# A hybrid decoder layer: adaLN weight loads on GpSimd's queue, and early-tile biases by one VectorE pass each over transposed weights, paused around two stages

## The chip, the cores and the metric

The kernel runs on one core of one Trainium2 chip. The metric is the device time of one execution in microseconds (us); the number given for a kernel is the median of three runs. Most executions of a kernel agree within 0.3%.

## The reference

One layer, one sequence of 512 tokens, width 2048, all in float32:

```python
mod = silu(c) @ w_ada + b_ada                       # w_ada is 2048 x 6144
shift, scale, gate = split(mod, 3)
h = rms_norm(x, norm_w) * (1 + scale) + shift
proj = h @ w_in                                     # q, k, v, gates, DeltaNet q/k/v, z, beta, a, merge gates
y_a = (sliding_window_attention(...) * silu(ag)) @ w_o_swa
y_b = (gated_delta_rule(...) normed * silu(z)) @ w_o_dn          # w_o_dn is 4096 x 2048
y = sigmoid(mg_a) * y_a + sigmoid(mg_b) * y_b
out = x + gate * (y @ w_out)
```

Only `c` and `w_ada` are needed for `shift`, `scale` and `gate`. The product `h @ w_in` splits into `(norm(x)*(1+scale)) @ w_in + shift @ w_in`, and the second term is one number per output channel: a bias.

## The kernel before, in words

**Matmuls.** A weight tile of 128 output channels (`raw`, 128x2048, 1 MB) is loaded by SP's queue (`load_job`, L203). `split` (L53) makes a high part on ACT (`whi`, L55) and a low part on DVE (`wlo`, L56), half a tile at a time, and `mm3` (L243 to L245) does three matmuls of 128x512 per 128 input channels: high by high, high by low, low by high. The hidden state lies in SBUF as `hh` and `hl`. `channel_tile` does one such tile: 48 matmuls, with a call of `pump` after every sixth.

**Startup (L345 to L555).** The four `x` tiles are loaded (L367). Thirty-two tiles of `w_ada` (`wa`, 1 MB each, six buffers that the `x` tiles use too) are loaded by SP (L359), and each gives 128 values of `scale` (the first 16) or `shift` (the last 16), in `ada_sum`: for tiles 0, 1, 23, 25, 27 and 29 by matmuls on PE (L413, L419), otherwise by one DVE pass (L422). `high` makes the hidden channels (ACT L443, L444) and `low` their remainder (DVE L448).

The projections begin before the shift is known. In the loop over the 16 blocks of input channels nine output tiles at once (two value tiles `v`, seven tiles `b` of the branch-b merge gate; weights `w_st`) are made from the state without shift, so they lack their bias. `store` copies each out of PSUM on ACT (L514) and SP writes it to DRAM (L515). Two more unshifted tiles follow (mb5 and mb6, here called so by their place), and beside them the last twelve `ada_sum`s, stepped by `pump`. Then the whole state is made again with the shift (DVE L438, ACT L444, DVE L448), and the tile `ba` (weights `w_tr`, with a `k` tile beside it) is the first that uses it.

**Order.** A tile scheduler turns the program into one queue of instructions per engine, and each engine runs its queue in order. Next to the tiles, generators are stepped by `pump`: those in `live` with a delay, those in `slow` with a budget (the first DeltaNet solve, `s0`, 0.88 per call), and those in `side` at a rate per call.

**Branch b (L1033 to L1070).** For each half of 4096 channels the DeltaNet output is read back from DRAM in 16 tiles (`oraw`, two buffers, L1048) and split into `oh` (ACT L55) and `ol` (DVE L56); meanwhile PE does two merge-gate tiles, and then 16 tiles `od` follow. Side work at rate 0.36 comes first from `shift_products`, then from `gate`. `shift_products` makes the missing biases of the nine early tiles: it loads the same weights again (`sw`, L1532; for the first tiles in pieces of 512 bytes a packet), multiplies by the shift on POOL (L1537), sums over the 16 blocks on DVE (L1542) and over partitions by a 128x1 matmul (L1545, L1548). `gate` loads 16 tiles `gw` (L1561) and accumulates them on DVE (L1567), then sums over partitions on PE (L1575) and DVE (L1576). Both share one buffer for `sw` and `gw`.

Of the kernel before, what the change touches and what calls it, by code (L numbers as in the profile page):

```python
# [7 lines left out]
F32 = mybir.dt.float32  # L8
# [8 lines left out]
P = 128  # L17
# [22 lines left out]
class Layer:  # L40
# [239 lines left out]
    def build(self):  # L280
        tc, nc, a = self.tc, self.nc, self.a
        with ExitStack() as es:
# [12 lines left out]
            self.hold, self.keep_order = 0, False  # L295
# [49 lines left out]
    def startup(self, st):  # L345
# [9 lines left out]
        def load_ada(n):  # L355
            if n >= 2 * KT:
                return
            wa = s2.tile([P, D], F32, tag="wa", name="wa", bufs=6)
            nc.sync.dma_start(out=wa, in_=a["w_ada_ss"][n // KT, n % KT])  # L359
            loads[n] = wa  # L360
# [151 lines left out]
        def store(ps, dst):  # L512
            t = s2.tile([P, T], F32, tag="h32", name="raw")
            nc.scalar.copy(out=t, in_=ps)  # L514
            nc.sync.dma_start(out=dst, in_=t)  # L515
# [128 lines left out]
    def deltanet(self):  # L644
# [9 lines left out]
        with ExitStack() as ps:  # L654
# [4 lines left out]
            with ExitStack() as sa:  # L659
# [9 lines left out]
                s0 = self.paced(self.solve(sol0, 0, nc.vector), 0.88)  # L669
# [363 lines left out]
    def branch_b(self):  # L1033
        tc, nc, a = self.tc, self.nc, self.a
        with ExitStack() as es:
# [5 lines left out]
            self.beside(self.shift_products(wk, pg), 0.36, "gate")  # L1041
            self.beside(self.gate(wk, pg), 0.36, "gate")
            oh = op.tile([P, KT, T], F32R, name="oh")
            ol = op.tile([P, KT, T], F32R, name="ol")
            for half in range(2):
# [6 lines left out]
                for j in range(KT):  # L1052
                    ps = self.channel_tile(f"od{half}_{j}", oh, ol)
                    y = wk.tile([P, T], F32, tag="yb", name="yb", bufs=3)
                    if half == 0:
                        nc.scalar.copy(out=y, in_=ps)
                    else:
# [3 lines left out]
                        if j < NPRE:  # L1061
                            nc.scalar.activation(th, th, AF.Tanh, scale=0.5, bias=self.bias_h[:, j : j + 1])
# [54 lines left out]
    def attention(self):  # L1117
        tc, nc, a = self.tc, self.nc, self.a
        with ExitStack() as es:
# [7 lines left out]
            for i in range(2):  # L1127
                t = keep.tile([P, T], F32, name=f"vch{i}")
                nc.sync.dma_start(out=t, in_=self.v_d[i])
                nc.scalar.activation(t, t, AF.Identity, bias=self.bias_v[:, i : i + 1])  # L1130
# [388 lines left out]
    def shift_products(self, wk, pp):  # L1519

        nc, a = self.nc, self.a
        st = a["w_st"].rearrange("u p (b c) -> p u b c", b=2)
        src = [st[:, :, :, i * P : (i + 1) * P] for i in range(2 + NST)] + [a["w_ch"][96 + j] for j in range(NST, NPRE)]
        ps = pp.tile([P, T], F32, tag="g", name="pshift")
        for _ in range(7):
            yield
        for n, w_d in enumerate(src):
            w = wk.tile([P, D], F32, tag="gw", name="sw", bufs=1)
            if n < 2 + NST:
                wb = w.rearrange("p (u b c) -> p u b c", b=2, c=P)  # L1530
                for b in range(2):
                    nc.sync.dma_start(out=wb[:, :, b, :], in_=w_d[:, :, b, :])  # L1532
            else:
                nc.sync.dma_start(out=w, in_=w_d)
            yield
            wv = w.rearrange("p (k c) -> p k c", c=P)
            nc.gpsimd.tensor_tensor(  # L1537
                out=wv, in0=wv, in1=self.shift.unsqueeze(2).to_broadcast([P, KT, P]), op=ALU.mult
            )
            yield  # L1540
            r = wk.tile([P, P], F32, tag="sr", name="sr", bufs=2)
            nc.vector.tensor_reduce(out=r, in_=w.rearrange("p (k c) -> p c k", c=P), axis=AX.X, op=ALU.add)  # L1542
            yield
            if n:
                nc.tensor.matmul(ps[:, n - 1 : n], lhsT=last, rhs=self.ones[:, 0:1], start=True, stop=True)  # L1545
            last = r
        yield
        nc.tensor.matmul(ps[:, n : n + 1], lhsT=last, rhs=self.ones[:, 0:1], start=True, stop=True)  # L1548
        self.bias_v = self.const.tile([P, 2], F32, name="bias_v")
        nc.vector.tensor_copy(out=self.bias_v, in_=ps[:, 0:2])  # L1550
        self.bias_h = self.const.tile([P, NPRE], F32, name="bias_h")
        nc.vector.tensor_scalar(out=self.bias_h, in0=ps[:, 2 : 2 + NPRE], scalar1=0.5, scalar2=None, op0=ALU.mult)
        yield

    def gate(self, wk, pp):

        nc, a = self.nc, self.a
        acc = wk.tile([P, D], F32, name="gate_bc", bufs=1)
# [23 lines left out]
def layout(i):  # L1582
# [21 lines left out]
    o["w_ch"] = f(np.concatenate([ch(w_in[:, 4608:16896]), ch(w_in[:, 19008:]), ch(w_in[:, :2304]), ch(w_in[:, 2560:4608]), ch(w_in[:, 16960:19008])]))  # L1604
    o["w_os"] = f(ch(i["w_o_swa"][0]))
# [57 lines left out]
```

## Time and profile before

| what | value |
|---|---|
| median of 3 runs | 2981.06 us (2978.43 to 2982.47) |
| profiled execution | 2980.36 us |
| its span in the trace | 2978.6 us |
| PE busy | 2887.3 us (97%) |
| DVE, ACT, POOL busy | 1858.3, 1099.8, 272.8 us |
| DMA | 460.57 MB, mean 155 GB/s |

A row of a group reads: line, engine, operation, result and operands, shape, count, then busy time, mean duration, and the time for which the engine sat idle just before, with what ended it. Matmuls overlap in the pipe, so that the duration of one (some 0.39 us) is longer than the distance between the starts of two.

### The profile page before, as it was taken

Reading aid. Unit: us, or ns where it says so; the run is one execution under the profiler, and the core shown is the slowest. Engines: PE = TensorE matmul, PEld = TensorE weight load, DVE = VectorE, ACT = ScalarE, POOL = GpSimd, SP = SyncE. Lnnn points to the kernel's source line nnn. Section 1 sums busy time; section 2 is a strip of 40 time slices with the busy share of each in tenths; the row PEclk is TensorE's granted clock in tenths of the full one; section 3 lists DMA queues with packets and bytes.
Section 4 is the critical chain, followed back from the end, with each engine's and each line's share of the span. In section 5 each row is a group of like instructions: output and inputs, shape, how many; then the busy total and the mean of one; then the engine's idle time right before and its main releaser. Section 6 shows DMA issues by size and latency. Waiting matters only on the chain.

```text
span 2978.6 us, 38106 instructions
## 1 busy us (share of the span) xinstructions
PE 2887.3 (97%) x14506; PEld 2362.3 (79%) x14506; DVE 1858.3 (62%) x2962; ACT 1099.8 (37%) x2136; POOL 272.8 (9%) x213
## 2 busy tenths in 40 slices
PE   8888999899999999999999989999999999999988
PEld 7767788788888888888888778788788878778867
DVE  7676799677777544555554454553656556554697
ACT  5244433334334433333333322321234434432333
POOL 0002121121000000001000021000000000000011
PEclk9989999999999999999999999999999999999999
DMA  9746654643333533343332556865332223275563
GB/s 365 280 145 183 185 165 158 195 129 119 120 123 111 160 107 125 112 133 116 125 115 96 170 187 216 277 228 169 105 112 86 88 90 99 95 248 179 183 193 92
DMA packets 189897, 460.57 MB, mean 155 GB/s; under 512 B 72689, under 2 KB 89585, under 8 KB 153745
## 3 DMA queue, kind: packets, MB, share of 16 engines
q1 hardware_dynamic: 189714, 458.14, 46.6%
q8 instruction: 114, 1.87, 0.3%
q14 instruction: 69, 0.57, 0.1%
HBM read 396.39 MB, written 59.45 MB: 153 GB/s over the span
## 4 chain that ended last, share of the span: by engine, by line
PE 75%; DVE 7%; DMA 5%; issue 2%; ACT 2%; POOL 1%; SPq 0%; POOLq 0%; DVEq 0%; ACTq 0%
PE mm L243 21%; PE mm L245 21%; PE mm L244 21%; DMA oraw<-o_d 2%; DMA gw<-in_w_ada_gate 2%; DVE wlo L56 2%; PE S L1264 1%; PE pv L969 1%; PE po L988 1%; PE O L1315 1%; PE pP L277 1%; PE po L987 1%; PE pd L984 1%; PE pp L959 1%; DVE sr L1542 1%
## 5 line engine op out<-in xcount | busy, mean ns | idle before, releaser
L243 PE MATMUL mm<-hh,whi 128*128 128x512 f32 x2752 | 1120.5, 407 | 6.4 <-DVE yq L634 5.5
L245 PE MATMUL mm<-hh,wlo 128*128 128x512 f32 x2752 | 1079.7, 392 | 1.8 <-DVE wlo L56 1.8
L244 PE MATMUL mm<-hl,whi 128*128 128x512 f32 x2752 | 1077.4, 392 | 0.2 <-DVE hl L56 0.2
L56 DVE TENSOR_TENSOR wlo<-raw,whi 128x1024 fp32r<-128x1024 f32 (+1 forms) x452 | 559.9, 1242 | 449.8 <-ACT whi L55 445.2
L55 ACT CAST whi<-raw 128x1024 fp32r<-128x1024 f32 (+1 forms) x452 | 470.4, 1043 | 961.0 <-PE mm L244 874.8
L243 PEld LDWEIGHTS mm<-hh,whi 128*128 128x128 f32 x2752 | 519.7, 189 | 114.6 <-issue 14.3
L245 PEld LDWEIGHTS mm<-hh,wlo 128*128 128x128 f32 x2752 | 517.6, 188 | 114.3 <-DVE wlo L56 2.6
L244 PEld LDWEIGHTS mm<-hl,whi 128*128 128x128 f32 x2752 | 519.6, 189 | 98.8 <-issue 0.8
L244 PE MATMUL mm<-ol,whi 128*128 128x512 f32 x512 | 202.5, 397 | 6.3 <-DVE ol L56 6.3
L243 PE MATMUL mm<-oh,whi 128*128 128x512 f32 x512 | 203.5, 399 | 3.8 <-ACT oh L55 3.8
L245 PE MATMUL mm<-oh,wlo 128*128 128x512 f32 x512 | 201.8, 396 | 4.9 <-DVE wlo L56 4.9
L916 POOL TENSOR_TENSOR qe<-qe,yq 128x512 f32<-128x512 f32 x32 | 50.7, 1602 | 904.0 <-DMA qe<-eg_rows 786.4
L765 POOL TENSOR_TENSOR E<-E,neg_g 128x512 f32<-128x512 f32 x64 | 79.7, 1247 | 519.3 <-DMA E<-g_rows 262.5
L244 PEld LDWEIGHTS mm<-ol,whi 128*128 128x128 f32 x512 | 97.6, 191 | 31.0 <-DVE ol L56 10.1
L245 PEld LDWEIGHTS mm<-oh,wlo 128*128 128x128 f32 x512 | 97.7, 191 | 27.2 <-DVE wlo L56 7.1
L243 PEld LDWEIGHTS mm<-oh,whi 128*128 128x128 f32 x512 | 97.3, 190 | 26.5 <-ACT oh L55 5.4
L808 DVE TENSOR_TENSOR atmp<-A 128x62 f32<-128x62 f32 (+30 forms) x124 | 111.0, 895 | 1.4
L815 DVE TENSOR_TENSOR A<-A,atmp 128x62 f32<-128x62 f32 (+30 forms) x124 | 110.9, 894 | 1.5
L962 DVE SCALAR_TENSOR_TENSOR r<-pp,neg_eg,vt 128x128 f32<-128x128 f32 x96 | 29.2, 346 | 78.9 <-PE pp L959 77.6
L1288 ACT ACTIVATE sm<-sm,mx,rs 128x256 f32<-128x256 f32 (+1 forms) x128 | 71.7, 562 | 3.9 <-DVE mx L1283 3.9
L634 DVE SCALAR_TENSOR_TENSOR yv<-mm,convh,yv 128x511 f32<-128x511 f32 (+2 forms) x96 | 71.4, 744 | 1.6
L422 DVE SCALAR_TENSOR_TENSOR wa<-wa,silu_cb 128x2048 f32<-128x2048 f32 x26 | 59.4, 2284 | 5.9 <-DMA wa<-in_w_ada_ss 5.9
(351 smaller groups left out, 3320.6 us busy)
## 6 DMA issues: line engine op xcount, KB each, us to landing
raw<-in_w_ch SPq DMA_DIRECT2D x156, 1024.0 KB
wa<-in_w_ada_ss SPq DMA_DIRECT2D x32, 1024.0 KB
raw<-in_w_od SPq DMA_DIRECT2D x32, 1024.0 KB
E<-g_rows SPq DMA_DIRECT2D x64, 256.0 KB
gw<-in_w_ada_gate SPq DMA_DIRECT2D x16, 1024.0 KB
raw<-in_w_os SPq DMA_DIRECT2D x16, 1024.0 KB
qe<-eg_rows SPq DMA_DIRECT2D x32, 256.0 KB
o_d<-zh SPq DMA_DIRECT2D x32, 256.0 KB
```

What stands on the lines that cost most here:

```text
L55: self.nc.scalar.copy(out=hi, in_=src)
L56: self.nc.vector.tensor_tensor(out=lo, in0=src, in1=hi.bitcast(F32), op=ALU.subtract)
L243: nc.tensor.matmul(ps, lhsT=wh, rhs=xh, start=first, stop=False)
L244: nc.tensor.matmul(ps, lhsT=wh, rhs=xl, start=False, stop=False)
L245: self.last_mm = nc.tensor.matmul(ps, lhsT=wl, rhs=xh, start=False, stop=last).ins
L422: nc.vector.scalar_tensor_tensor(out=wa, in0=wa, scalar=1.0, in1=scb, op0=ALU.mult, op1=ALU.mult, accum_out=acc)
L634: nc.vector.scalar_tensor_tensor(out=y[:, s:], in0=ps[:, : T - s], scalar=w[:, j : j + 1], in1=y[:, s:], op0=ALU.mult, op1=ALU.add)
L765: nc.gpsimd.tensor_tensor(out=E, in0=E, in1=ng, op=ALU.add)
L808: eng.tensor_tensor(out=t, in0=A[:, m : m + 1, m + 1 :].to_broadcast([P, m, n]), in1=A[:, :m, m : m + 1].to_broadcast([P, m, n]), op=ALU.mult,
L815: eng.tensor_tensor(out=A[:, :m, m + 1 :], in0=A[:, :m, m + 1 :], in1=t, op=ALU.add)
L916: nc.gpsimd.tensor_tensor(out=qf, in0=qf, in1=q, op=ALU.mult)
L1288: nc.scalar.activation(t, t, AF.Exp, scale=r[:, h : h + 1], bias=mx[:, h : h + 1], accum_out=den[:, h : h + 1])
```

## The change

1. The 32 loads of `wa` are issued by GpSimd (POOL) and not by SP.
2. The nine stores of early tiles are issued by ACT and not by SP.
3. The budget of `s0` is 0.85 for 0.88.
4. `pump` skips side work while a flag `side_held` is set: from the start of branch b until its first tile `od0_0` has been done, and from `od0_15` until `od1_0` has been done. Between, the rate is 0.28 for 0.36.
5. `shift_products` is another computation. Sixteen 128x128 matmuls and four ACT copies spread the shift as a row over all partitions (`row`, in the buffer that `gate` accumulates in afterwards). Then each of the nine tiles is loaded from a copy of the weights with output channels on partitions (`w_early`, 128x2048, 8 KB in a row), and one DVE pass multiplies by the row and accumulates to one column of `bias`. POOL's multiplications, DVE's reductions and the 128x1 matmuls are gone.

```diff
@@ pump
-            if not q:
+            if not q or self.side_held:
                 continue
@@ startup: load_ada, store
-            nc.sync.dma_start(out=wa, in_=a["w_ada_ss"][n // KT, n % KT])
+            nc.gpsimd.dma_start(out=wa, in_=a["w_ada_ss"][n // KT, n % KT])
...
-            nc.sync.dma_start(out=dst, in_=t)
+            nc.scalar.dma_start(out=dst, in_=t)
@@ deltanet
-                s0 = self.paced(self.solve(sol0, 0, nc.vector), 0.88)
+                s0 = self.paced(self.solve(sol0, 0, nc.vector), 0.85)
@@ branch_b
-            self.beside(self.shift_products(wk, pg), 0.36, "gate")
-            self.beside(self.gate(wk, pg), 0.36, "gate")
+            row = wk.tile([P, D], F32, name="gate_bc", bufs=1)
+            self.beside(self.shift_products(wk, pg, row), 0.28, "gate")
+            self.beside(self.gate(wk, pg, row), 0.28, "gate")
...
+            self.side_held = True
...
                     ps = self.channel_tile(f"od{half}_{j}", oh, ol)
+                    self.side_held = j == KT - 1
@@ shift_products
+        for q in range(4):
+            ps = pp.tile([P, 4, P], F32, tag="g", name="pshift")
+            for c in range(4):
+                w = self.shift[:, 4 * q + c : 4 * q + c + 1].to_broadcast([P, P])
+                nc.tensor.matmul(ps[:, c, :], lhsT=w, rhs=self.ident, start=True, stop=True)
+            nc.scalar.copy(out=row[:, q * T : (q + 1) * T], in_=ps.rearrange("p c n -> p (c n)"))
             yield
+        bias = self.bias = self.const.tile([P, 2 + NPRE], F32, name="bias")
+        for n in range(2 + NPRE):
             w = wk.tile([P, D], F32, tag="gw", name="sw", bufs=1)
+            nc.sync.dma_start(out=w, in_=a["w_early"][n])
             yield
+            nc.vector.scalar_tensor_tensor(
+                out=w, in0=w, scalar=1.0, in1=row, op0=ALU.mult, op1=ALU.mult, accum_out=bias[:, n : n + 1]
+            )
             yield
```

Rows of the order read: line, operation, result and operands, shape, and how many follow each other. The first place is startup. Here is SP's queue of the kernel before at the end of the loop over the 16 blocks; `wa` are the adaLN tiles, `raw` of L203 the weights of coming tiles, `v_d` and `mb_d` the stores of early tiles:

```order
L203 DMA raw<-in_w_ch 128x2048
L359 DMA wa<-in_w_ada_ss 128x2048 x4
L515 DMA v_d<-raw 128x512 x2
L203 DMA raw<-in_w_tr 128x1536
L515 DMA mb_d<-raw 128x512 x2
L359 DMA wa<-in_w_ada_ss 128x2048
L515 DMA mb_d<-raw 128x512 x2
L359 DMA wa<-in_w_ada_ss 128x2048
L515 DMA mb_d<-raw 128x512
L359 DMA wa<-in_w_ada_ss 128x2048 x3
```

Now SP's queue in startup holds weights alone, from its sixth row on:

```order
L203 DMA raw<-in_w_st 128x1792 x2
L338 DMA convh<-in_conv_w 128x256
L326 DMA dnw<-in_dn_norm_w 128x1
L203 DMA raw<-in_w_st 128x1792 x6
L203 DMA raw<-in_w_ch 128x2048 x2
L203 DMA raw<-in_w_tr 128x1536 x2
L203 DMA raw<-in_w_ch 128x2048 x3
```

The stores went to ACT's queue, and all 32 loads of `wa` stand in a row in POOL's, ahead of its first work on `E` (L765). On ACT itself, in the same loop, the casts `whi` of the next weights stood behind several blocks of hidden channels (`h_...` and `hh`) in a row before:

```order
L55 COPY whi<-raw 128x896
L443 ACTIVATE h_511<-xnT,scale 128x512
L55 COPY whi<-raw 128x896
L444 COPY hh<-h_511 128x512
L443 ACTIVATE h_545<-xnT,scale 128x512
L444 COPY hh<-h_545 128x512
L443 ACTIVATE h_581<-xnT,scale 128x512
L444 COPY hh<-h_581 128x512
L443 ACTIVATE h_615<-xnT,scale 128x512
L444 COPY hh<-h_615 128x512
L443 ACTIVATE h_651<-xnT,scale 128x512
L444 COPY hh<-h_651 128x512
```

Now a cast follows each one or two blocks:

```order
L443 ACTIVATE h_511<-xnT,scale 128x512
L444 COPY hh<-h_511 128x512
L55 COPY whi<-raw 128x896
L443 ACTIVATE h_545<-xnT,scale 128x512
L444 COPY hh<-h_545 128x512
L55 COPY whi<-raw 128x896
L443 ACTIVATE h_581<-xnT,scale 128x512
L444 COPY hh<-h_581 128x512
L55 COPY whi<-raw 128x896
L443 ACTIVATE h_615<-xnT,scale 128x512
```

PE's queue has all four late `ada` groups (tiles 23, 25, 27, 29) inside mb5 and mb6; before, two of the four stood behind mb6. The second place is the beginning of branch b, on DVE. Before, the reductions of `shift_products` (L1542) stood between the splits `ol` of the read-back tiles:

```order
L56 TENSOR_TENSOR ol<-oraw,oh 128x512
L1542 TENSOR_REDUCE sr<-sw 128x128
L56 TENSOR_TENSOR ol<-oraw,oh 128x512
L56 TENSOR_TENSOR wlo<-raw,whi 128x1024
L56 TENSOR_TENSOR ol<-oraw,oh 128x512 x2
L56 TENSOR_TENSOR wlo<-raw,whi 128x1024
L56 TENSOR_TENSOR ol<-oraw,oh 128x512 x2
L1542 TENSOR_REDUCE sr<-sw 128x128
L56 TENSOR_TENSOR wlo<-raw,whi 128x1024
L56 TENSOR_TENSOR ol<-oraw,oh 128x512 x3
L1542 TENSOR_REDUCE sr<-sw 128x128
```

Now the first pass of `shift_products` (L1537) comes behind the last of the sixteen `ol`:

```order
L56 TENSOR_TENSOR ol<-oraw,oh 128x512 x2
L56 TENSOR_TENSOR wlo<-raw,whi 128x1024
L56 TENSOR_TENSOR ol<-oraw,oh 128x512 x6
L56 TENSOR_TENSOR wlo<-raw,whi 128x1024 x3
L1537 TENSOR_SCALAR sw,bias<-sw,gate_bc 128x2048
L56 TENSOR_TENSOR wlo<-raw,whi 128x1024 x2
L1537 TENSOR_SCALAR sw,bias<-sw,gate_bc 128x2048
```

On SP the same: of the nine loads of `sw` one still stands among the first half's sixteen loads of `oraw`, where there were eight of the half-tile pieces of `sw` before. In the second half three loads of `gw` stand between the first `oraw` and the last, as before, and three loads of `yb` that stood behind them now stand among them.

More of the change, by code (lines that the diff above doesn't have):

```diff
@@ L1517, in output, with shift_products @@
             evict(*f)
-    def shift_products(self, wk, pp):
+    def shift_products(self, wk, pp, row):
         nc, a = self.nc, self.a
[L1522 to L1525, printed above, removed]
+        for q in range(4):
[4 more added lines that the diff above has]
+            nc.scalar.copy(out=row[:, q * T : (q + 1) * T], in_=ps.rearrange("p c n -> p (c n)"))
@@ L1543, in shift_products @@
[L1543 to L1552, printed above, removed]
@@ L1553, in shift_products, with gate @@
-        yield
-    def gate(self, wk, pp):
+        nc.vector.tensor_scalar(out=bias[:, 2:], in0=bias[:, 2:], scalar1=0.5, scalar2=None, op0=ALU.mult)
+    def gate(self, wk, pp, acc):
         nc, a = self.nc, self.a
-        acc = wk.tile([P, D], F32, name="gate_bc", bufs=1)
         for kt in range(KT):
```

20 lines of the change are left out of this document (5 added, 15 removed).

## The prediction

> **What bounds the kernel now.** The page comes first: its busy times, and the granted clock in the forty slices.
>
> ```profile
> PE 2887.3 (97%) x14506; PEld 2362.3 (79%) x14506; DVE 1858.3 (62%) x2962; ACT 1099.8 (37%) x2136; POOL 272.8 (9%) x213
> PEclk9989999999999999999999999999999999999999
> DMA  9746654643333533343332556865332223275563
> ```
>
> PE is busy 97% of the span, so what an edit can win is PE's idle time, some 90 us, and what it can cost is work put into PE's stream. The change touches two stages, startup and branch b. I cut the span there and read PE's busy time and its count of matmuls in each stretch. The columns are the stretch, its length, then busy time and count of PE, PEld, DVE, ACT and POOL, the granted clock, the DMA share and GB/s.
>
> ```profile
> 28.50:58.50 30.00, 29.99 (x159) 24.47 (x160) 26.66 (x38) 13.03 (x19) 0.00 (x0) 1.00 1.01 415
> 58.50:70.00 11.50, 8.59 (x25) 6.21 (x24) 11.46 (x15) 6.82 (x10) 0.00 (x0) 0.70 0.66 261
> 70.00:112.50 42.50, 42.50 (x189) 35.21 (x188) 35.41 (x43) 15.71 (x21) 0.00 (x0) 1.00 0.86 344
> 112.50:137.40 24.90, 24.90 (x166) 19.66 (x164) 11.95 (x16) 6.16 (x10) 0.00 (x0) 1.00 0.40 137
> 137.40:158.80 21.40, 5.09 (x69) 4.03 (x68) 8.25 (x12) 2.88 (x6) 0.00 (x0) 0.56 0.99 381
> 158.80:186.20 27.40, 26.09 (x98) 17.16 (x99) 24.06 (x39) 12.47 (x21) 0.00 (x0) 0.84 0.26 84
> ...
> 1697.00:1740.00 43.00, 33.49 (x127) 24.83 (x125) 25.99 (x19) 10.84 (x15) 7.53 (x3) 0.92 0.60 183
> 1740.00:1885.00 145.00, 143.04 (x637) 118.21 (x636) 75.02 (x41) 37.71 (x46) 22.18 (x6) 1.00 0.63 216
> 1885.00:1940.00 55.00, 47.85 (x187) 36.11 (x186) 34.55 (x33) 17.84 (x25) 0.00 (x0) 0.94 0.83 292
> ```
>
> The stretch from 70 to 112.5 has no gap: 42.5 us for 189 matmuls, 0.225 us each. At that pace the others should last 25 x 0.225 = 5.6 (a loss of 5.9 us), 98 x 0.225 = 22.0 (5.4), 127 x 0.225 = 28.6 (14.4), 637 x 0.225 = 143.3 (1.7) and 187 x 0.225 = 42.1 (12.9). From 137.4 to 158.8 only matmuls of `ada` run, and all 21.4 us are lost. Together 61.7 us lie where the change reaches.
>
> Why the 21.4? Windows of 10 us around it, and what SP's queue did there:
>
> ```profile
> 120.00:130.00 10.00, 10.00 (x73) 7.92 (x73) 5.36 (x8) 0.75 (x2) 0.00 (x0) 1.00 0.07 27
> 130.00:140.00 10.00, 7.45 (x61) 5.52 (x59) 2.41 (x4) 3.29 (x6) 0.00 (x0) 1.00 0.63 204
> 140.00:150.00 10.00, 2.52 (x34) 2.01 (x34) 3.86 (x5) 2.02 (x4) 0.00 (x0) 0.50 0.96 351
> ```
>
> ```profile
> 126.38 7.02 SPq L515 DMA_DIRECT2D mb_d<-raw  x2
> 133.51 0.37 SPq L359 DMA_DIRECT2D wa<-in_w_ada_ss  x1
> 135.03 1.41 SPq L515 DMA_DIRECT2D mb_d<-raw  x2
> 136.53 0.46 SPq L359 DMA_DIRECT2D wa<-in_w_ada_ss  x1
> 140.79 0.32 SPq L515 DMA_DIRECT2D mb_d<-raw  x1
> 141.20 1.36 SPq L359 DMA_DIRECT2D wa<-in_w_ada_ss  x3
> ```
>
> From 120 to 130 the DMA engines stood at 0.07 while PE was full: SP held the stores of early tiles, which wait for ACT's copy, and the `wa` loads behind them could not be issued. When they were (133 to 145), PE had run out. So the queue's order made this gap, not the bytes. The waits over startup (engine and line, what it waited for, us in total, times, longest) say the same for SP, and those of PE name what came late:
>
> ```profile
> SPq L515 <- ACT raw L514: 31.4, 7, 15.5
> ...
> PE ada L413 <- DMA wa<-in_w_ada_ss: 12.0, 2, 6.0
> PE v L243 <- ACT whi L55: 1.9, 1, 1.9
> ...
> POOL E L765 <- DVE ss L713: 214.7, 1, 214.7
> ```
>
> **The change part by part**, against the profiled execution (2980.36 us; its span is 2978.6, and the median of the three runs, 2981.06, lies 0.7 above it).
>
> *The start.* With `wa` on a second queue its first two tiles come beside the four `x` tiles, 2 MB more at 0.415 MB/us (the window at share 1.01): up to 4.8 us later for the last `x`. But an `x` tile costs PE some 3.7 us and the chain is PE's and ACT's:
>
> ```profile
> 15.82 7.38 PE L471 MATMUL xtp<-dg,xt 128*128 128x128 f32 x64 [0.59 <-ACT xnT L476]
> 17.47 1.91 ACT L456 ACTIVATE hl<-xt 128x2048 fp32r<-128x2048 f32 x1
> ```
>
> ACT took the last `x` at 17.47, when four MB from 3 us on had been due at about 13. So 4 us of the delay are covered: I take +1.5, between 0 and +5.
>
> *58.5 to 70.* PE waits here for casts of weights, which stood on ACT behind five blocks of hidden channels; those wait for the `scale`s of late `wa`. Weights and `wa` now have queues of their own, and casts alternate with blocks. DVE was busy 11.46 of 11.5 here and 26.66 of 30 ahead of it, so part of the loss can stay on DVE: per block it owes one pass of `ada_sum`, a remainder and one split of 896 columns.
>
> ```profile
> L56 DVE TENSOR_TENSOR wlo<-raw,whi 128x1024 fp32r<-128x1024 f32 (+1 forms) x452 | 559.9, 1242 | 449.8 <-ACT whi L55 445.2
> ...
> L422 DVE SCALAR_TENSOR_TENSOR wa<-wa,silu_cb 128x2048 f32<-128x2048 f32 x26 | 59.4, 2284 | 5.9 <-DMA wa<-in_w_ada_ss 5.9
> ```
>
> That is 2.28 and 1.24 x 896 / 1024 = 1.09, with 0.69 for the remainder (row below) and some 0.3 of small pieces, 4.4 us, against 21 matmuls x 0.225 = 4.7 on PE: it fits, with little over. I take -4.5 (0 to -5.9).
>
> *Two groups of `ada` move ahead*, into mb5 and mb6. Before, they ran in the gap, where they cost nothing. One group shifts the stream around it by 1.1 us, and its column sum by some 0.4 (four starts late by 0.1 each), so +3.0 for two (2.2 to 3.4):
>
> ```profile
> 130.83 0.39 PE L245 MATMUL mm<-hh,wlo 128*128 128x512 f32 x1
> 131.15 1.08 PE L413 MATMUL ada<-wa,silu_cr 128*32 128x128 f32 x32
> 132.16 0.50 PE L243 MATMUL mm<-hh,whi 128*128 128x512 f32 x1
> ```
>
> *The gap.* Up to the tile `ba` startup loads 36 tiles of `wa` and `x` (1.05 MB), 8 of `w_st` (0.92), 2 of `w_ch` and 2 of `w_tr` (0.79), 48.8 MB; at 0.415 MB/us that is 118 us, ahead of mb6's end near 137. A `wa` also needs a free buffer: the last one takes that of the sixth sum before it, in the middle of mb6, near 126, and lands near 130. DVE must do eight passes of 2.28 us beside mb5 and mb6 (18 of 25 us, with four more in place of the gap's), which fits by little. What then stays is the way from the last sum through DVE (0.54), ACT (0.62) and PE (rows below): 2 us. So -19.4, between -12 (the last sums spill over by three DVE passes and a landing) and -21.4.
>
> *The tile `ba`.* Its 27.4 us hold 24.06 us of DVE, that is the rebuilt state:
>
> ```profile
> L448 DVE TENSOR_TENSOR hl<-h,hh 128x512 fp32r<-128x512 f32 x16 | 10.4, 686 | 1.5 <-ACT hh L444 1.5
> ...
> L438 DVE TENSOR_SCALAR h<-xnT,scale,shift 128x512 f32<-128x512 f32 x16 | 8.1, 540 | 0.0
> ...
> L444 ACT CAST hh<-h 128x512 fp32r<-128x512 f32 x16 | 9.3, 617 | 12.3 <-DVE h L438 12.3
> ```
>
> DVE can't do this much faster than 24, but a part of it may begin under mb6, and the clock need not recover from 0.56. I take -2.5 (0 to -5).
>
> *The stores on ACT* take its queue some 0.4 us each (row at 140.79: 0.32), 3.6 us in all, where ACT has 6.16 busy of 24.9; uncovered they would delay casts by those 3.6. *POOL's 32 loads* stand ahead of its first multiplication, which waits until 214.7 us anyway, long after the last load: nothing.
>
> *Branch b, first half.* The loss of 14.4 belongs to the read-back tiles, for which ACT and behind it DVE wait:
>
> ```profile
> ACT oh L55 <- DMA oraw<-o_d: 29.0, 11, 8.3
> ...
> L55 ACT CAST oh<-oraw 128x512 fp32r<-128x512 f32 x32 | 19.7, 620 | 58.8 <-DMA oraw<-o_d 58.6
> ...
> L1542 DVE TENSOR_REDUCE sr<-sw 128x128 f32<-128x2048 f32 x9 | 34.2, 3802 | 25.5 <-POOL sw L1537 24.1 <-PE pshift L1545 1.4
> L1567 DVE SCALAR_TENSOR_TENSOR gate_bc<-gw,silu_c,gate_bc 128x2048 f32<-128x2048 f32 x12 | 28.2, 2352 | 35.5 <-DMA gw<-in_w_ada_gate 35.5
> ```
>
> Three reductions of 3.8 us stood between the `ol`, and eight pieces of `sw` between the loads; all but one load go. Eight pairs of `oraw` with two buffers then take perhaps 3.7 us each (0.5 MB at 0.415, two casts of 0.62, and the issue), 30 us, while PE has two merge tiles (21.6) and then follows block by block: about 3 us of loss stay. Sixteen fp32 matmuls for the shift row are new on PE: 32 passes, at 7.38 / 64 each, 3.7 us. So -14.4 + 3 + 3.7 = -8 (-3 to -12). *Between the halves* nine DVE passes (2.28 by the nearest row, of `wa`, or 2.35 by the one above) replace nine of 3.80, but nothing waits for them: 0 (-2 to +2). *Second half.* The scheduler puts three `gw` loads and three DVE passes between the `oraw` as before, and three `yb` loads (0.75 MB) more, so the pause is not one in the queues: -1 (-5 to +5).
>
> *The solve at 0.85* moves steps by at most half a tile and ends in the same phase: 0 (-2 to +3).
>
> Sum: 1.5 - 4.5 + 3.0 - 19.4 - 2.5 - 8 - 1 = -30.9, and 2980.4 - 30.9 = **2949.5 us**.
>
> **The rivals.**
>
> *Bytes, not order.* If the transfers of both queues only share what one queue had, the idle 0.93 of the window from 120 to 130 (9.3 us) is all that comes back of the gap, and the loss at 58.5 stays: 1.5 + 3.0 - 9.3 - 8 - 1 = -13.8, 2966.6 us. Against it: the share of 0.07. For it: shares of 1.01 and 0.99 on either side. The Trainium skill, in "DMA: Bandwidth & Descriptors", section "Issuing engines are not separate DMA queues", speaks for it: transfers issued by any engine run on the same 16 DMA engines and interleave, and a second issuer saves only the time to initiate, usually small. The row of 31.4 us on SP disagrees in this kernel: what is saved is the wait of an issue that blocks others.
>
> *Slower: loads from POOL come one at a time.* The trace has no load from POOL. If each of the 32 takes T us from 3 us on, with no overlap, the last lands at 3 + 32 T. Before it landed near 156, so T = 4.8 gives the old gap, and with the 9 us of branch b the kernel breaks even at T = 5.1. At T = 6 the last lands at 195, +39 on the gap: 2980.4 + 39 - 9 = 3010 us. Against it: 1 MB is 2.4 us at 0.415 MB/us, so T must be double. For it: the loads have to share with as many bytes of weights. On the price there are two statements in the Trainium skill. "DMA: Bandwidth & Descriptors", section "Anatomy of one DMA — SWDGE (gpsimd) path", fits 2.0 us plus the bytes at 436 GB/s for one load from GpSimd, an estimated 4.4 us here; one at a time that gives 144 for the last and about 2957 us. "SBUF — State Buffer", section "SBUF: two separate sides", warns that GpSimd can't write descriptors while DVE runs a two-port operation; DVE's work here is mostly two-input passes (L422, L448, L56), and no run so far shows the effect.
>
> *Branch b gives nothing.* The one `sw` load and `yb`, `gw` loads keep their place, two buffers of `oraw` are slow by themselves, and the shift row costs its 3.7: 2949.5 + 9 = 2958.5. For it: the second half, with no `sw` at all, lost 12.9 us, and half of the 58.6 us that `oh` waited fell there.
>
> *All stalls go.* The gap closes entirely (2 more), the loss at 58.5 and in `ba` too (1.4 and 2.5), the start costs nothing (1.5), and branch b loses nothing (3, and 5 in the second half): 2949.5 - 15.4 = 2934.
>
> **How the numbers follow.** Forecast 0.48, branch b nothing 0.18, all stalls go 0.15, bytes 0.12, one at a time 0.07. The range of 2932 to 2968 us takes in the first four but for their tails (0.10), and leaves out the last: 0.83 inside. About 0.2%, or 6 us, is what a measurement of this kernel can tell from no change. Faster by more 0.88 (the first four but 0.05), within it 0.05, slower 0.07.
>
> **What would show it.** In the trace after: no row of SP that waits for L514; the DMA share from 120 to 130 well over 0.07, and PE without a gap of over 5 us between the last early tile and `ba`; the loss near 60 us under 2 us; 16 `oh` casts of the first half waiting less than 15 us for `oraw` in place of 29. I am wrong if `wa` loads land over 4.8 us apart, if the gap stays over 10 us with the DMA engines full, or if DVE is what PE waits for beside mb5 and mb6.

## The result, and the profile after

The changed kernel took 2958.54 us (median of 4 runs, 2954.88 to 2960.22) against 2980.34 us before (4 runs): a ratio of 0.9925, with a 95% interval of 0.9908 to 0.9942. That is 21.8 us faster, where 30.9 were forecast. The profiled execution took 2958.96 us, its span is 2957.2.

PE's time is the page's first row again, with 3.7 us less busy time and 21.4 us less span:

```profile
PE 2883.6 (98%) x14520; PEld 2362.0 (80%) x14520; DVE 1834.1 (62%) x2970; ACT 1105.7 (37%) x2140; POOL 244.9 (8%) x236
```

The same stretches as in the prediction, cut at the same events in the new trace (columns as there):

```profile
0.00:35.00 35.00, 25.36 (x226) 24.33 (x226) 19.34 (x76) 19.57 (x28) 4.45 (x12) 0.90 0.93 357
35.00:111.50 76.50, 76.50 (x345) 63.24 (x339) 76.03 (x96) 35.24 (x48) 11.85 (x23) 1.00 1.00 404
111.50:122.60 11.10, 11.10 (x78) 8.89 (x76) 5.55 (x7) 2.21 (x3) 1.06 (x2) 1.00 1.02 414
122.60:131.50 8.90, 0.42 (x3) 0.05 (x1) 1.22 (x2) 2.99 (x6) 0.00 (x0) 0.79 0.58 218
131.50:150.90 19.40, 19.40 (x156) 14.64 (x156) 7.83 (x14) 2.96 (x6) 0.00 (x0) 0.83 0.36 122
150.90:177.10 26.20, 24.28 (x102) 15.79 (x101) 21.91 (x36) 13.69 (x22) 0.00 (x0) 1.00 0.25 79
...
1693.60:1726.60 33.00, 30.89 (x146) 24.61 (x145) 12.72 (x15) 14.18 (x22) 0.00 (x0) 1.00 0.59 193
1726.60:1868.60 142.00, 142.00 (x632) 117.75 (x631) 72.68 (x56) 36.52 (x44) 0.00 (x0) 1.00 0.71 249
1868.60:1920.00 51.40, 46.65 (x193) 37.58 (x192) 29.18 (x28) 17.97 (x25) 0.00 (x0) 0.93 0.85 299
```

The loop over input channels now starts at 35 us and not at 28.5, and runs to 111.5 without a gap, with the DMA engines (1.00) and DVE (76.03 of 76.5) full. Of the gap of 21.4 us ahead of `ba` some 2 us are left. But a new one has come, 8.9 us inside mb5, followed by a slow clock (0.83). The first half of branch b loses little now: at 0.225 us each its 146 matmuls come to 32.9 of its 33.0 us.

To see where time was won and given back I compared the start of the same matmul in both traces. Each column is an event; the first row is its time before, the second how much later (+) or earlier (-) it came after:

| | first `v` | end of loop | end of mb6 | first `ba` | last `ba` | near 600 | first `od` | 4th `od` tile | end of half 1 | start of half 2's tiles | end of branch b |
|---|---|---|---|---|---|---|---|---|---|---|---|
| before, us | 28.5 | 112.3 | 137.1 | 158.9 | 184.6 | 598.7 | 1697.0 | 1745.6 | 1887.6 | 1947.3 | 2102.5 |
| after | +6.5 | -1.0 | +13.8 | -6.0 | -9.1 | -3.3 | -3.4 | -12.7 | -17.9 | -21.4 | -21.4 |

So startup won 9.1 us, the DeltaNet stage gave 5.8 back, and branch b won 18.

**The start.** ACT's first two passes over `x` wait longer, and PE's transposes with them. ACT of the changed kernel:

```profile
9.75 1.91 ACT L456 ACTIVATE hl<-xt 128x2048 fp32r<-128x2048 f32 x1 [6.83 <-DMA xt<-in_x]
...
14.45 1.91 ACT L456 ACTIVATE hl<-xt 128x2048 fp32r<-128x2048 f32 x1 [1.25 <-DMA xt<-in_x]
```

The first pass came at 6.89 before, so the first `x` tile explains 2.9 of the 6.5 us. PE meanwhile ran out of other work, stood for 4.6 us from 9.6 on, and its clock fell. PE from 10 to 20 us, before and after:

```profile
10.00:20.00 10.00, 9.04 (x77) 8.68 (x76) 7.38 (x38) 8.62 (x12) 0.00 (x0) 1.00 1.03 421
10.00:20.00 10.00, 5.75 (x32) 5.65 (x32) 4.37 (x24) 8.58 (x12) 0.00 (x0) 0.66 1.02 418
```

**The new gap.** PE's queue and ACT's at that place. Each row is start, duration, engine, line, and in brackets the idle time before with what ended it:

```profile
122.24 0.50 PE L243 MATMUL mm<-hh,whi 128*128 128x512 f32 x1
122.58 0.40 PE L244 MATMUL mm<-hl,whi 128*128 128x512 f32 x1
131.45 0.59 PE L419 MATMUL ada<-pick,adas 128*128 128x1 f32 x2 [8.47 <-ACT adas L418]
```

```profile
108.41 0.35 ACTq L515 DMA_DIRECT2D v_d<-raw  x1
108.80 0.59 ACT L514 COPY raw<-v 128x512 f32<-128x512 f32 x1 [0.42 <-PE v L245]
109.41 0.33 ACTq L515 DMA_DIRECT2D v_d<-raw  x1
116.76 0.59 ACT L514 COPY raw<-b 128x512 f32<-128x512 f32 x1 [7.38 <-DMA v_d<-raw]
...
122.04 0.59 ACT L514 COPY raw<-b 128x512 f32<-128x512 f32 x1 [3.15 <-DMA v_d<-raw]
...
128.17 0.59 ACT L514 COPY raw<-b 128x512 f32<-128x512 f32 x1 [3.09 <-DMA mb_d<-raw]
...
131.13 0.27 ACT L418 COPY adas<-ada 128x128 f32<-128x128 f32 x1 [0.40 <-ACT raw L514]
```

The issue of a store costs ACT 0.33 us, as costed. But the copies have two buffers, and the third copy waits for the first store to land: issued at 108.41, landed by 116.76, while the loads of both other queues fill the DMA engines (1.02). ACT takes its instructions in order, so the small copy `adas`, ready at 122.3, stands until 131.13 behind the copy that has just begun, three more of them and one cast, and PE stands behind `adas`.

**GpSimd's loads.** One takes POOL 0.53 us to issue, and they overlap: the median is 9.1 us from issue to landing, and at the end of the loop they go out 2.2 to 3.5 us apart.

```profile
92.45 0.53 POOL L359 DMA_DIRECT2D wa<-in_w_ada_ss  x1 [3.41 <-DVE wa L422]
94.66 0.53 POOL L359 DMA_DIRECT2D wa<-in_w_ada_ss  x1 [1.68 <-DVE wa L422]
98.12 0.53 POOL L359 DMA_DIRECT2D wa<-in_w_ada_ss  x1 [2.93 <-DVE wa L422]
```

In the loop nearly all of POOL's waiting (62.9 us in 21 waits) is for DVE to free a buffer. So the rival of loads one at a time (4.8 us each and more) is out.

**Branch b.** The reductions of 3.8 us have become passes of 2.29, and in the first half (1680 to 1740) ACT waits 9.2 us for read-back tiles in place of 29.0:

```profile
L56 DVE TENSOR_TENSOR ol<-oraw,oh 128x512 fp32r<-128x512 f32 x32 | 21.2, 689 | 21.6 <-ACT oh L55 21.6
L1537 DVE SCALAR_TENSOR_TENSOR sw<-sw,gate_bc 128x2048 f32<-128x2048 f32 x9 | 20.6, 2291 | 18.0 <-DMA sw<-in_w_early 14.5 <-ACT gate_bc L1530 3.5
```

```profile
ACT whi L55 <- PE mm L244: 21.9, 9, 4.7
ACT oh L55 <- DMA oraw<-o_d: 9.2, 5, 2.9
```

The mean of `ol` itself went from 838 to 689 ns. But no `ol` of before took 838: thirty took 0.67 to 0.69 us, as now, and two took 3.26 and 2.96. This is the second of them, on DVE of the kernel before:

```profile
1726.77 2.96 DVE L56 TENSOR_TENSOR ol<-oraw,oh 128x512 fp32r<-128x512 f32 x1 [4.99 <-ACT oh L55]
1729.65 3.79 DVE L1542 TENSOR_REDUCE sr<-sw 128x128 f32<-128x2048 f32 x1
```

POOL multiplied for the old bias from 1725.57 to 1729.18 and, beside the other one, from 1692.92 to 1697.30. Three passes `wlo` met such a multiplication too, and took 2.86 to 3.79 us for 1.22. All five ended the same time behind POOL's end, 0.55 us for `ol` and 1.08 for `wlo`, whenever they had begun: in this trace a DVE pass of these kinds stands still until POOL's instruction has ended. The same holds, with the same 0.55 and 1.08 us, for all five such meetings in each of four runs below that keep the old computation (startup only, `wa` on GpSimd only, stores on ACT only, pause only). PE's waits from 1680 to 1740, of which 4.5 us were for `ol` before, have shrunk to one of 2.1:

```profile
PE mm L244 <- DVE ol L56: 4.5, 4, 1.5
```

```profile
PE mm L243 <- ACT oh L55: 2.1, 1, 2.1
```

### The profile page after: what moved, and what is told of

The parts are those of the page before. It is cut to its first block, busy times and chain, and to the rows that moved or that the text cites. A ratio compares the mean times of both kernels' runs of the same rounds, so it can differ in the third digit from the quotient of the medians.

```text
span 2957.2 us, 38131 instructions
## 1 busy us (share of the span) xinstructions
PE 2883.6 (98%) x14520; PEld 2362.0 (80%) x14520; DVE 1834.1 (62%) x2970; ACT 1105.7 (37%) x2140; POOL 244.9 (8%) x236
## 4 chain that ended last, share of the span: by engine, by line
PE 79%; DVE 6%; DMA 3%; ACT 2%; issue 1%; POOL 1%; SPq 0%; POOLq 0%; DVEq 0%; ACTq 0%
PE mm L243 23%; PE mm L245 22%; PE mm L244 22%; DVE wlo L56 2%; DMA oraw<-o_d 1%; PE S L1267 1%; PE pv L969 1%; PE po L988 1%; PE O L1318 1%; PE pP L277 1%; PE pd L984 1%; PE pp L959 1%; PE po L987 1%; DMA qe<-eg_rows 1%; PE m L244 0%
## 5 line engine op out<-in xcount | busy, mean ns | idle before, releaser
L56 DVE TENSOR_TENSOR wlo<-raw,whi 128x1024 fp32r<-128x1024 f32 (+1 forms) x452 | 552.4, 1224 | 470.1 <-ACT whi L55 445.8
L243 PEld LDWEIGHTS mm<-hh,whi 128*128 128x128 f32 x2752 | 520.9, 189 | 116.7 <-issue 15.2
L765 POOL TENSOR_TENSOR E<-E,neg_g 128x512 f32<-128x512 f32 x64 | 76.5, 1196 | 404.3 <-DMA E<-g_rows 266.8
```

The lines of the kernel that those rows point to most:

```text
L56: self.nc.vector.tensor_tensor(out=lo, in0=src, in1=hi.bitcast(F32), op=ALU.subtract)
L243: nc.tensor.matmul(ps, lhsT=wh, rhs=xh, start=first, stop=False)
L765: nc.gpsimd.tensor_tensor(out=E, in0=E, in1=ng, op=ALU.add)
```

## The experiments

The theories. A: startup lost what was missing to two new stalls, `x` sharing the transfer rate with the first adaLN tiles, and ACT's queue standing at copies that wait for stores to land. B: the stall in mb5 is one of late adaLN tiles. C: the start is late since a load from GpSimd is slow by itself. D and E: the DeltaNet stage gave 5.8 us back by chance of the clock, or through the solve budget of 0.85. F and G: branch b won by the cheaper bias computation, or by the pauses. Medians before were 2981.03, 2980.59 and 2981.17 us in the three groups of runs. The table gives the same landmarks, in us against the profile before:

| | us, ratio [interval] | first `v` | end of loop | end of mb6 | last `ba` | near 600 | end of branch b |
|---|---|---|---|---|---|---|---|
| the change | 2958.54, 0.9925 [0.9908, 0.9942] | +6.5 | -1.0 | +13.8 | -9.1 | -3.3 | -21.4 |
| own store buffers | 2954.15, 0.9910 [0.9896, 0.9924] | +6.2 | -1.4 | +7.3 | -15.6 | -11.0 | -26.1 |
| five `wa` buffers | 2957.97, 0.9923 [0.9910, 0.9937] | +6.3 | -1.2 | +11.8 | -10.5 | -8.8 | -27.2 |
| first two `wa` by SP | 2956.66, 0.9919 [0.9905, 0.9933] | +1.6 | -4.2 | +11.6 | -11.3 | -9.9 | -27.9 |
| branch b only | 2960.61, 0.9938 [0.9925, 0.9952] | -0.1 | -1.4 | -1.4 | -2.6 | -2.2 | -24.3 |
| startup only | 2972.42, 0.9981 [0.9972, 0.9990] | +6.4 | -1.1 | +13.4 | -9.0 | -9.6 | -8.1 |
| `wa` on GpSimd only | 2970.50, 0.9971 [0.9959, 0.9982] | +7.2 | -0.3 | +12.1 | -9.4 | -10.9 | -11.0 |
| stores on ACT only | 2972.59, 0.9976 [0.9966, 0.9985] | +0.1 | +0.3 | +4.3 | -6.2 | -9.8 | -12.2 |
| both repairs | 2943.22, 0.9876 [0.9862, 0.9889] | +0.1 | -5.8 | +3.2 | -19.7 | -15.2 | -36.2 |
| budget 0.88 | 2953.86, 0.9915 [0.9902, 0.9927] | +7.1 | -0.4 | +13.9 | -9.0 | -10.2 | -26.4 |
| both repairs, 0.88 | 2940.16, 0.9865 [0.9851, 0.9879] | -0.3 | -6.2 | +0.3 | -22.1 | -23.1 | -42.7 |
| new bias, no pause | 2964.69, 0.9948 [0.9934, 0.9962] | +0.1 | -1.1 | -1.1 | -1.6 | +1.4 | -14.5 |
| pause only | 2978.61, 0.9997 [0.9989, 1.0006] | -0.2 | -1.3 | -1.4 | -2.3 | -1.8 | -3.1 |

Unchanged stages differ by up to 3 us between profiles, so differences of less in a column prove nothing alone. Single runs of one kernel differ by 2 to 15 us, and a profile is one run: those of branch b only and of the first two `wa` by SP lay 6.8 and 4.7 us under their medians.

**Own store buffers, and its control.** In the changed kernel:

```diff
+            own = len(stored) % 3 < 2
+            stored.append(0)
-            t = s2.tile([P, T], F32, tag="h32", name="raw")
+            t = s2.tile([P, T], F32, tag="st" if own else "h32", name="raw", bufs=4 if own else 2)
...
-            wa = s2.tile([P, D], F32, tag="wa", name="wa", bufs=6)
+            wa = s2.tile([P, D], F32, tag="wa", name="wa", bufs=5)
```

> The changed kernel, with six buffers for the nine stores of early tiles (four of their own and the two they had) and, since SBUF has no room for them beside it, five buffers for the adaLN tiles in place of six. Theory A: the stall of 8.9 us behind 122.6 us comes from ACT's queue, which stands still at the copies of the early tiles until earlier stores have landed (7.4 us the longest), so that the small copy that PE waits for comes late. With more buffers the stall goes, and the slow clock behind it: 2945 to 2950 us, the wait of PE on the copy of ada under 1 us. Theory B: PE waits because the last adaLN tiles and their DVE passes are late; then the stall stays or grows with one buffer less: 2958 to 2965 us.

The control has the last two lines alone (and the same for `xt`).

> The changed kernel with five buffers for the adaLN tiles in place of six, and nothing else: the control of the run with own store buffers. Theory A: the second adaLN tile is loaded only when the first x tile is free, so the start has less beside it and gains some 2 us, while the stall behind 122.6 us stays: 2954 to 2960 us. Theory B (late adaLN tiles): the depth of the loads is what counts, 2962 us or more.

With its own buffers ACT reaches `adas` at 121.96, and PE's wait for it is not in the list any more. What is left there is another wait, of PE for DVE, to free the one PSUM tile of `ada`:

```profile
PE ada L413 <- DVE shift L431: 3.8, 2, 3.6
PE ba L243 <- ACT hh L444: 1.7, 1, 1.7
PE mm L245 <- DVE wlo L56: 1.6, 1, 1.6
```

In the control it stands as in the changed kernel:

```profile
PE ada L419 <- ACT adas L418: 6.9, 1, 6.9
PE ba L243 <- ACT hh L444: 1.7, 1, 1.7
```

So theory A holds for this stall, and B falls for it, since one buffer less for adaLN tiles did not make it worse. But the wait that is left is of theory B's kind. DVE of the run with own store buffers:

```profile
131.52 2.29 DVE L422 SCALAR_TENSOR_TENSOR wa<-wa,silu_cb 128x2048 f32<-128x2048 f32 x1 [4.43 <-DMA wa<-in_w_ada_ss]
...
134.73 0.21 DVE L431 TENSOR_SCALAR shift<-ada,b_adaT 128x1 f32<-128x1 f32 x1
```

The pass that frees the tile stands on DVE behind one that waits for a late adaLN tile. With five buffers the last two tiles landed at 131.5 and 135.6, and at 124.5 and 127.5 in the changed kernel, so this may be the price of the buffers taken. From the end of the loop to that of mb6 the time fell from +14.8 to +8.7 us, the control's is +13.0. The total was 2954.15, short of the 2945 to 2950 expected: of the 11.8 us over the forecast (+3.0) the stores had 6.1, and late adaLN tiles stand next in line. The control's total fits theory A, but not the 2 us at the start that it had promised.

**First two adaLN loads by SP**, in the changed kernel:

```diff
-            nc.gpsimd.dma_start(out=wa, in_=a["w_ada_ss"][n // KT, n % KT])
+            (nc.sync if n < 2 else nc.gpsimd).dma_start(out=wa, in_=a["w_ada_ss"][n // KT, n % KT])
```

> The changed kernel with the first two of the 32 adaLN loads issued by SP behind the x tiles, as before, and the other thirty by GpSimd. Theory A: the first projection matmul came 6.5 us later than before (35.1 us) since two adaLN tiles took half the transfer rate from the x tiles; it comes back to 28 to 30 us. If the loop over input channels is bound by what it has to load (DMA share 1.0), it gives a part back: 2953 to 2958 us. Theory C: the late start is one of GpSimd's slower first loads and not of sharing: then the first matmul stays near 35 us and the time at 2958.

The first `v` came at +1.6 us for +6.5, and the loop's end at -4.2 for -1.0, so two thirds of it lasted: the late start was the order of the first loads. The edit alone does not part sharing from slow first loads of GpSimd (theory C), since both go with it, but the traces do. In the changed kernel GpSimd's first two tiles landed at 9.30 and 14.25, and PE needs the first at 27.7; what came late was `x`. The control with five buffers has only one adaLN tile beside the `x` tiles and still started at +6.3: its first `x` came at 9.36, PE stood for 3.7 us, and from 10 to 20 the clock was 0.66 there too (0.83 with the first two loads by SP). So theory A holds, but the second adaLN tile adds little: one beside the first `x` is enough to run PE dry and slow its clock. The median, 2956.66, lies in theory A's range and can't be told from the changed kernel's by itself.

**Both parts of startup, together and apart**, each on the kernel before:

> The kernel before with the two edits of startup alone: all 32 adaLN loads by GpSimd, the nine stores by ACT; branch b and the solve budget as before. Theory A (the startup edits win 9 us by the end of the tile ba and the stages behind them keep that, since they are the same code): 2971 us. Theory D (part of it is given back in the DeltaNet stage, where gaps of PE of some 3 us lie otherwise against the times at which the clock is judged; the changed kernel lost 5.7 us of 9 there): 2975 to 2980 us, with the granted clock under 1.00 somewhere between 230 and 400 us.

> The kernel before with the 32 adaLN loads by GpSimd alone; the nine stores stay on SP. Theory A: ACT's copies still wait for the landing of earlier stores, and SP's stores wait for ACT's copies with weights queued behind them, so a stall between the early tiles stays: the gap ahead of ba is short, the stall near 122 us between 4 and 12 us, 2968 to 2976 us. Rival: with no store on ACT the stall near 122 us is gone, and the gap ahead of ba too: 2962 to 2966 us.

> The kernel before with the nine stores by ACT alone; all loads stay on SP. Theory A: SP no longer stands still between 112 and 140 us, so the adaLN loads come early and most of the gap of 21.4 us closes, with no extra load beside the x tiles at the start: 2960 to 2968 us. Rival: what closed the gap is the second queue for loads, and without it the adaLN loads stand behind weights of later tiles as before: 2975 to 2982 us.

Together they won 8.2 us, apart 10.1 and 8.0: either edit alone does what both do. Startup only came out by theory A (2971), not D (2975 to 2980): its -9.0 at the last `ba` is -9.6 near 600. With the stores on ACT and all loads still on SP, the first two stores land in 4 us and not 8, SP no longer waits for ACT's copies, and the loads come early (the DMA share from 120 to 130 is 1.01, where it was 0.07); so it isn't the second queue for loads that closed the gap, but that a store which waits no longer stands ahead of loads. They are not free of the stores, though: four loads of `wa` still waited 23.8 us in all on SP for events that the profile puts down to landings of `mb_d`; why is not shown. With the loads alone on GpSimd the wait for `adas` stays (6.7 us), since ACT's copies wait for landings whoever issues them: the rival of 2962 to 2966 failed. Theory A's own figure for the stores alone (2960 to 2968) was too good as well: the gap ahead of `ba` closed to 2 us (from +4.3 at the end of mb6 to -15.4 at the first `ba`), but the tile itself then waited for its state and gave 9 us back (-6.2 at its end). PE in that stretch:

```profile
PE ba L243 <- ACT hh L444: 5.7, 2, 5.0
PE ada L419 <- ACT adas L418: 2.2, 1, 2.2
```

**Branch b only** is the change without its startup edits and with the budget of 0.88.

> The kernel before with the new bias computation, the pauses and the rate 0.28 alone; loads and stores in startup by SP, solve budget 0.88. By the traces branch b gained 11.5 us in the first half, 3 between the halves and 4 in the second, some 18 us: 2962 us. If part of that came from the other phase of the DeltaNet stage behind the changed startup, it is less: 2966 to 2972 us.

It won 20.4 us, nearly all of the change's gain, and a little more than the 2962 expected. With startup only (8.2) that makes 28.6, and the change with the budget at 0.88 won 27.3: the two parts add up.

**Budget 0.88**, in the changed kernel and in the one with both repairs:

```diff
-                s0 = self.paced(self.solve(sol0, 0, nc.vector), 0.85)
+                s0 = self.paced(self.solve(sol0, 0, nc.vector), 0.88)
```

> The changed kernel with the solve budget back at 0.88 and nothing else. In the profiles, the five kernels with 0.85 lost between 1.4 and 5.8 us against the kernel before from the end of the tile ba to 600 us, and the four with 0.88 lost 0.4 or won up to 3.6. Theory E (the budget of 0.85 costs this): 2953 to 2956 us, no loss in that stage. Theory D (the loss is chance, by where gaps lie against the times at which the clock is judged): 2956 to 2960 us, no difference to the changed kernel that the runs can tell.

> The changed kernel with both repairs: first two adaLN loads by SP behind the x tiles, and six buffers for stores (with five for the adaLN tiles). Theory A: the 6.5 us at the start come down to 1 to 2 and the stall near 122 us to under 3; the two repairs gave 1.9 and 4.4 us by themselves, so 2950 to 2953 us. Theory D: the traces show more won in startup (over 15 us against before by the end of ba) than stays at the end of the DeltaNet stage.

> Both repairs of startup and the solve budget at 0.88. Theory E: some 4 us under both repairs with 0.85 (2943.2), 2938 to 2940 us. Theory D: 2941 to 2945 us.

With 0.88 the stage behind `ba` gives nothing back (-9.0 to -10.2, and -22.1 to -23.1), with 0.85 it gives 5.8 and 4.5. The medians say the same way, -4.7 and -3.1 us (2953.86 lies in theory E's range, 2940.16 just above it), though each pair's intervals overlap; two other kernels with 0.85 lost only 1.4 and 1.7 there, and one with 0.88 (new bias, no pause) lost 3.0. The traces part the theories. From the last `ba` to the event near 600 the time is PE's idle time, what slow clock cost (one minus the granted clock, summed), and a rest, which is work at full clock. Before, these were 20.5, 6.8 and 386.4 us; in the change 21.1, 10.2 and 388.2. The rest is 387.2 to 388.2 us in all five kernels with 0.85 and 385.4 to 386.6 in all nine with 0.88: some 2 us go with the budget (theory E). The cost of the slow clock does not go with it: 6.8 us in two kernels with 0.85 and in most with 0.88, 10.2 in the change and own store buffers, and 10.2 too in the new bias without pause (theory D). So of the change's 5.8 us some 3.4 are clock, 1.8 work and 0.6 idle time.

Both repairs won 15.3 us over the change, more than their sum apart (6.3) and than the 2950 to 2953 expected: 2943.22, and 2940.16 with 0.88, which beat the kernel before and the change by clear intervals. In the profiles 10.6 us of that stand at the last `ba`, where the two apart have 6.5 and 2.2; the remainder comes behind it, in code that the repairs don't touch, and is not explained.

**Bias and pause apart**, each on the kernel before; without the pause the two lines on `side_held` in branch b are left out, and the pause alone is those lines with the old bias computation.

> The kernel before with the new bias computation and the rate 0.28, without the pauses; startup and solve budget as before. Theory F (the first half of branch b was slow since side work, its 512-byte packets and the 3.8 us reductions on DVE above all, stood between the read-back tiles; contiguous loads and shorter passes alone take most of that away): 2962 to 2966 us. Rival G (any side work between the read-back tiles costs, so the pause is what pays): 2970 to 2978 us.

> The kernel before with the pauses alone: the old bias computation on POOL, DVE and PE at its rate of 0.36, held back until the first tile of each half has been done. Rival G (the pause is what pays): 2962 to 2968 us. Theory F: the old work, moved behind the read-back, slows the tiles there, 2970 to 2978 us.

The new computation alone won 16.5 us of the 20.4, as theory F expected. The pause alone won nothing that can be told (its 2978.61 lies just outside theory F's range and far from G's). But it did not test rival G fairly: the scheduler put the old reductions back between the `ol`, so that the pause moved none of them away, and in the new kernel without pause three of the new passes stand there too. DVE of the pause alone, 1680 to 1740:

```profile
L56 DVE TENSOR_TENSOR ol<-oraw,oh 128x512 fp32r<-128x512 f32 x16 | 15.2, 967 | 11.6 <-ACT oh L55 11.6
L1544 DVE TENSOR_REDUCE sr<-sw 128x128 f32<-128x2048 f32 x3 | 11.2, 3730 | 4.1 <-POOL sw L1539 4.1
```

and of the new bias without pause:

```profile
L1535 DVE SCALAR_TENSOR_TENSOR sw<-sw,gate_bc 128x2048 f32<-128x2048 f32 x5 | 11.5, 2290 | 7.0 <-DMA sw<-in_w_early 6.8
...
L56 DVE TENSOR_TENSOR ol<-oraw,oh 128x512 fp32r<-128x512 f32 x16 | 10.8, 690 | 10.0 <-ACT oh L55 10.0
```

The 967 ns are again a mean over fourteen `ol` of 0.67 to 0.69 us and two of 2.91 and 2.96 that met a multiplication of POOL. So the cheaper computation has a part that theory F did not name: with POOL's multiplications gone nothing holds DVE's splits. How much of the 16.5 us that is, apart from loads and reductions, no run tells. What the pause adds to the new computation is some 4 us (2964.69 to 2960.61), not clear of the intervals.

## Why the prediction was right, and where it was not

The direction, the place of the gains and the range held. The sum was 9 us too good, and its terms were off by more, in both directions: three came out 22.6 us worse than forecast and six 13.0 us better. That the total still lay in the range is in part luck.

| step | forecast | measured |
|---|---|---|
| the start | +1.5 (0 to +5) | +6.5 |
| loop | -4.5 | -7.5 |
| mb5 and mb6 | +3.0 | +14.8 |
| gap ahead of `ba` | -19.4 | -19.8 |
| tile `ba` | -2.5 | -3.1 |
| solve at 0.85 | 0 (-2 to +3) | +5.8 |
| branch b, first half | -8 | -9.3 |
| between the halves | 0 (-2 to +2) | -5.2 |
| second half | -1 | -3.5 |

The stretches are the prediction's: "first half" ends with the third `od` tile, "between the halves" is the remainder of the first half, and "second half" the read-back at its beginning. Of the signs that the prediction named one failed: PE has a gap of over 5 us between the last early tile and `ba`, the one in mb5. (The "about 2957 us" for loads one at a time at 4.4 us comes to 2959 by the same sum; nothing else hangs on it.)

*Gap.* Right, and for the reason given: no row of SP waits for L514 any more, and the DMA engines work at 1.02 until 122.6, where they had stood at 0.07.

*mb5 and mb6* is the step that failed. I costed the stores on ACT by what it takes to issue them (3.6 us in all) and looked for cover for that. What counted was their landing, 8.3 us for the first under full loads, with two buffers. The traces of before had it in small: the copies waited up to 4.1 us for `mb_d` there. The stall of 8.5 us and the slow clock behind it (0.83 over 19.4 us, 3.3 us) are the difference to +3.0.

*The start.* I took 4 of the 4.8 us as covered, since ACT took the last `x` 4 us late anyway. But the first `x` tile came late too (9.75 for 6.89), and each of the four goes through ACT, DVE and PE in turn, so the whole chain moved; and the prediction left out that PE, with nothing to do, would lose its clock (0.66 from 10 to 20). The loop made up for it better than forecast: with its loads early it had no gap at all.

*First half.* The size was nearly right, the working only in part: it counted the loads and the reductions among the `ol`, and left out that POOL's multiplications stop DVE's splits.

*Between the halves.* "Nothing waits for them" was wrong, and a term was left out. From the fourth `od` tile to the end of the half PE had stood idle for 3.2 us, in two waits for `wlo`, one of 2.0 behind a reduction and one of 1.2 behind a pass of `gate`; now it never stands. And PE's busy time fell by 2.0 us, from 138.8 to 136.8, since the twelve passes of the old 128x1 sums that lay there are gone. The prediction counted the new matmuls of the shift row and not these.

*The solve.* Put at nothing; it cost 5.8 us, in the shares above.

The Trainium skill, in "DMA: Bandwidth & Descriptors", section "Issuing engines are not separate DMA queues", says that DMAs of all issuers run on the same 16 engines, so that a second issuer saves only the time to initiate. The runs agree that a second issuer brings nothing by itself: loads alone on it (-10.1) did no better than stores alone off the first (-8.0), within what can be told. They differ in what is saved: not the time to initiate, but waiting in one queue, 31.4 us of SP's before. The Trainium skill, in "SBUF — State Buffer", section "SBUF: two separate sides", warns of loads from GpSimd that starve beside two-port operations of DVE. In the loop DVE was busy 76.03 of 76.5 us and the DMA share 1.00, so no starving is seen beside these passes; whether any of them is such an operation, the trace doesn't say.

## What to carry to other kernels

A store that is moved to another engine's queue takes its wait along: cost it by the landing under load and the number of buffers, not by the issue, and ask what else that engine owes to PE. When a waiting instruction blocks a queue, try moving either what waits or what stands behind it: here one was enough, and both together won no more. When the mean of a group has grown, look at its single instructions: here two of 32 had stood still behind another engine's work. And a pause in the code's order is worth only what the scheduler leaves of it, so read the order before believing in it.

## What was not expected of the hardware

Nearly the same gap of PE costs a slow clock in one run and none in another. In the changed kernel, windows of 2 us around a wait of the DeltaNet stage (the granted clock is the third column from the end):

```profile
272.00:274.00 2.00, 0.36 (x2) 0.00 (x0) 1.83 (x6) 0.00 (x0) 1.86 (x3) 1.00 0.00 0
274.00:276.00 2.00, 1.09 (x4) 0.91 (x5) 0.46 (x1) 1.15 (x4) 0.44 (x1) 0.62 0.00 0
276.00:278.00 2.00, 2.00 (x10) 1.74 (x9) 0.00 (x0) 0.82 (x3) 0.00 (x0) 0.53 0.35 131
```

and the same wait in the kernel before:

```profile
282.00:284.00 2.00, 0.20 (x1) 0.00 (x0) 1.90 (x4) 0.00 (x0) 1.92 (x3) 1.00 0.00 0
284.00:286.00 2.00, 1.15 (x8) 1.04 (x9) 0.32 (x3) 1.14 (x4) 0.00 (x0) 1.00 0.00 0
286.00:288.00 2.00, 2.00 (x12) 1.70 (x11) 0.00 (x0) 1.95 (x6) 0.00 (x0) 1.00 0.66 236
```

In the four us behind the gap 14 matmuls started, and 20 before. The gaps are 2.6 and 2.7 us long (272.36 to 274.91, and 282.20 to 284.85). What differs is where they lie. In all fourteen traces here the granted clock is 1.00 or 0.50 and nothing between, and within a trace it changes only on a grid of 3.41 us. In the changed kernel an edge of the grid falls at 274.49: in the 3.41 us ahead of it PE was idle for 2.1, and behind it the clock is 0.50 until 277.90. In the kernel before an edge falls at 283.43 and cuts the gap in two, 1.2 and 1.4 us, and nothing follows. Over all the traces (from 14 to 2900 us), of the grid's cells at full clock none with less than 1.45 us of idle PE was followed by a slow one, and each with over 1.93 was; in between both occur. So about half a cell decides.

The Trainium skill, "TensorE: Matmul & The Clock Gate", section "Part 1: The HAM clock gate (the "warmup" mystery)", states the grid: the clock is judged in free-running windows of some 3.4 us. The traces agree; where the page speaks of an idle window, some half of one was enough here. An edit that shifts all later gaps by a few us can so change the time of stages that it doesn't touch, as with 3.4 of the 5.8 us in the DeltaNet stage; that runs of one kernel differ by some us would follow too, but only one run of each was traced.
